# A transformer block on one core: six gates' combined weights kept in DRAM between two token blocks, and the side work of the last gates taken two steps at a time from an earlier product on

## The chip, the cores and the metric

The kernel runs on one core of one Trainium2 chip. The metric is the device time of one execution in microseconds (us). Before the change it is 3030.67 us, the median of three runs (3028.79 to 3031.12).

Engines are called as in the profile: PE (TensorE matmuls; PEld its weight loads), DVE (VectorE), ACT (ScalarE), POOL (GpSimd), SP (SyncE, which here only issues DMAs; ACT issues a few).

## The reference, cut to what matters

```python
h_x = modulate(x, norm1_g[l], sh1, sc1)                 # x: 2048 tokens x 1024
p_x = h_x @ w_in[l]                                     # w_in: 1024 x 3840, all f32
q_x, u_x, vg_x, ga_x, gb_x = jnp.split(p_x[..., KV_COLS:], REST_SPLITS, axis=-1)
...
gm_x = gmlp_spatial(jax.nn.gelu(u_x), jax.nn.gelu(vg_x), ...)
y = jax.nn.sigmoid(ga_logit) * (attn_o @ w_br_attn) + jax.nn.sigmoid(gb_logit) * (gm_o @ w_br_gm)
x = x + g1 * (y @ w_out[l])
```

The change lies in the projection `h_x @ w_in`, in its last 2048 columns, which give the two gates `ga` and `gb` (1024 columns each). Attention, the output projection and the squared-ReLU MLP come after it and are not touched.

## The kernel before, in words

**The projection.** The 2048 tokens are worked through in two token blocks of 1024 (`blk` 0 and 1, loop in `project`). Every block goes through two column pairs (`Pair`: keys, values and queries; then the gMLP's u and v) and then through eight gates (`Gate`, g = 0 to 7), each of 256 columns. Both are done by a Strassen-like scheme with seven half-size products in the order `SUMS = (0, 1, 5, 6, 4, 2, 3)`. The operands of a product are sums and differences of quarters of the block and of the weights. Every f32 operand is split in a high part `h` (rounded to fp32r) and a low part `l`, and a product is three matmuls for each 128 rows: h by h, h by l, l by h. A gate's product is 12 matmuls of 128x512 (`product`, L1609 to L1611).

**The weights of a gate.** `gate_weights(g, w)` is a generator that makes one gate's operands in steps. It loads the two 128-column halves r0 and r1 of `w_in` (L945, 512 KB each); splits r0 (ACT L954, DVE L955), which serves products 0 and 1; forms four differences (DVE L960 to L963); and splits these as two 128x1024 tiles (ACT L967, DVE L968), the first for products 5 and 3, the second for 4 and 6. Product 2's weights are loaded and split by `last_weights` (L2007, L2013, L2014) when products 5 and 6 run. The same weights serve both token blocks and are made anew in each.

**The order of the gates.** `gates` lays out the products of all gates of a run as one list: the first four products of a gate are interleaved with the last three of the gate before it. In block 1 all eight gates form one run; the list has 53 products, the first six gates in the way just told, the last two (g = 6 and 7) product by product in turn. With every product one step of the next gate's weight generator is taken, then the product is written out (`step`), then `tick` is called, once for each of the products 0 to 12 of the list and twice for each later one when `both` is true, which is in block 1 only. A gate's own evacuations are ACT copies and tanh and DVE additions on its PSUM bank (L2027, L2031, L2036, L2038, L2041, L2046, L2047); the results go to DRAM over SP (L2000). Gates 6 and 7 of block 1 keep their working tiles in the four slots named "m", all others in the eight slots named "t4".

**The side work.** `tick` takes one step of the first generator in `self.work`. These are `keys_work` (6 steps), `queries_work` (7 steps) and `mixing` (12 steps): normalization, rotary tables, gelu, the gMLP's spatial matmul (L182 to L184) and transposes, mostly on DVE and ACT. A mixing loads two tiles from DRAM (L791) into "m" slots, works on them (L802 to L833), splits (L149, L153), loads the spatial weights into an "m" slot (L839) and runs the matmuls. The "m" slots are four and one mixing fills them. In block 1 the list holds, behind what block 0 left, keys and queries of both halves and four mixings. After product 6 of gate 5 (`(g, p) == (KC - 3, 6)` in `ahead`) whatever is left of the list is written out at once. `tail` then brings in the first steps of attention (row maxima, L2100, L2106, L2111).

**Order on the engines.** The program is written with the Tile framework, whose scheduler orders each engine's instructions and hands out the slots of a tag; each engine and each DMA-issuing queue then works its instructions strictly in that order. So an instruction that waits holds up all that stand behind it on the same engine or queue.

Of the kernel before, what the change touches and what calls it, by code (L numbers as in the profile page):

```python
# [9 lines left out]
F32 = mybir.dt.float32  # L10
F32R = mybir.dt.float32r
I32 = mybir.dt.int32
AF = mybir.ActivationFunctionType
ALU = mybir.AluOpType
# [4 lines left out]
P = 128  # L19
D = 1024  # L20
KC = D // P
# [16 lines left out]
COL_GA = 1792  # L38
# [6 lines left out]
HK = KC // 2  # L45
# [5 lines left out]
def f32(ap):  # L51
    return ap.bitcast(F32)
# [10 lines left out]
}  # L63
SLOTS = {tag: n for tags in POOLS.values() for tag, n in tags.items()}
GROUP = 6
ON_VECTOR = (2, 4, 8, 14)
LAST_ON_VECTOR = (2, 4, 7, 8, 9, 12, 13, 14, 15)


class Kern:  # L70
# [119 lines left out]
    def constants(self):  # L190
        nc, I = self.nc, self.I
        ec = self.ctx.enter_context
        cp = ec(self.tc.tile_pool(name="const", bufs=1))
        dp = ec(self.tc.tile_pool(name="spill", bufs=1, space=DRAM))
        self.psum({"a": 4, "b": 4})
        self.ident = cp.tile([P, P], F32, name="ident")
        make_identity(nc, self.ident)
        self.ones = cp.tile([P, P], F32, name="ones")
        nc.vector.memset(self.ones, 1.0)
        self.lead = cp.tile([P, 1], F32, name="lead")  # L200
        nc.vector.memset(self.lead, 0.0)
        nc.vector.memset(self.lead[0:1], -1.0)
        self.G1 = cp.tile([P, KC, 2], F32, name="G1")
        self.S1 = cp.tile([P, KC, 2], F32, name="S1")
        self.G2 = cp.tile([P, KC], F32, name="G2")
        self.S2 = cp.tile([P, KC], F32, name="S2")
        self.silu = cp.tile([P, KC, 2], F32, name="silu")
        self.ss2 = cp.tile([P, SEQ // P], F32, name="ss2")
        self.gbs = cp.tile([P, GROUPS], F32, name="gbs")
        self.rg = {}  # L210
        for w in ("q", "k"):
            self.rg[w] = cp.tile([P, HD], F32, name=f"rg_{w}")

        def spill(n, shape):
            return [dp.tile(shape, F32, tag=f"{n}{b}", name=f"{n}_d{b}") for b in range(NB)]

        self.q_d = [
            [dp.tile([P, TB], F32, tag=f"q{b}_{p}", name=f"q_d{b}_{p}") for p in range(NH // 2)]
            for b in range(NB)
        ]  # L220
        self.gm_d = spill("gm", [512, TB])
        self.at_d = spill("at", [512, TB])
        self.ta_d = spill("ta", [D, TB])
        self.tb_d = spill("tb", [D, TB])
        self.x1_d = spill("x1", [TB, D])
        self.k_d = [
            [dp.tile([P, TB], F32, tag=f"k{c}_{v}", name=f"k_d{c}_{v}") for v in range(NKV)]
            for c in range(NB + 1)
        ]
        self.vc_d = dp.tile([P, TT, P], F32, tag="vc", name="vc_d")  # L230
        self.pr_d = [
            [
                [dp.tile([TB, n], F32, tag=f"p{n}_{b}_{j}", name=f"p{n}_d{b}_{j}") for j in range(2)]
                for b in range(NB)
            ]
            for n in (KVQ, TB)
        ]
        self.h_d = [
            [dp.tile([P, 2, TB], F32, tag=f"h{i}_{k}", name=f"h_d{i}_{k}") for k in range(HK)]
            for i in range(2)  # L240
        ]
        self.ws_d = [
            dp.tile([P, 2, TB], F32, tag=f"ws{c}", name=f"ws_d{c}") for c in range(2)
        ]
        self.t_d = [
            [
                [dp.tile([2, P, n], F32, tag=f"t{n}_{p}_{c}", name=f"t_d{n}_{p}_{c}") for c in range(2)]
                for p in range(7)
            ]
            for n in (KVQ, TB)  # L250
        ]

        def operands(n):
            return [
                [
                    dp.tile([2, P, TB], F32, tag=f"{n}{p}_{c}", name=f"{n}_d{p}_{c}")
                    for c in range(NCH)
                ]
                for p in range(7)
            ]  # L260

        self.ao_d = [operands(f"ao{blk}") for blk in range(2)]
        self.wo_d = operands("w2o")
        self.sm_d = spill("sm", [NH, TB])
        self.rs_d = spill("rs", [NH, TB])
        self.open("base")
        self.open("front")
# [615 lines left out]
    def context_keys(self):  # L883
# [52 lines left out]
        self.work += [self.keys_work(nt, None, kraw), self.gm_consts()]  # L936
        yield

    def gate_weights(self, g, w):
        nc = self.nc  # L940
        tt, sub = nc.vector.tensor_tensor, ALU.subtract
        lo = COL_GA + 2 * P * g
        r0, r1 = self.f4([KC, P]), self.f4([KC, P])
        for j, r in enumerate((r0, r1)):
            nc.sync.dma_start(  # L945
                r,
                self.I["w_in"][0][:, lo + j * P : lo + (j + 1) * P].rearrange(
                    "(k p) c -> p k c", p=P
                ),
            )  # L950
        b22 = r1[:, HK:]
        yield
        hr, lr = self.f4([KC, P], F32R), self.f4([KC, P], F32R)
        nc.scalar.copy(hr, r0)  # L954
        tt(out=lr, in0=r0, in1=f32(hr), op=sub)  # L955
        w[0] = [(hr[:, k], lr[:, k]) for k in range(HK)]
        w[1] = [(hr[:, HK + k], lr[:, HK + k]) for k in range(HK)]
        yield
        t13, t24 = self.f4([2, HK, P]), self.f4([2, HK, P])
        tt(out=t13[:, 0], in0=r1[:, :HK], in1=r0[:, :HK], op=sub)  # L960
        tt(out=t24[:, 0], in0=b22, in1=t13[:, 0], op=sub)
        tt(out=t13[:, 1], in0=b22, in1=r1[:, :HK], op=sub)
        tt(out=t24[:, 1], in0=r0[:, HK:], in1=t24[:, 0], op=sub)  # L963
        yield
        for alloc, t, ps in ((self.t4, t24, (5, 3)), (self.f4, t13, (4, 6))):
            h, l = alloc([2, HK, P], F32R), alloc([2, HK, P], F32R)
            nc.scalar.copy(h, t)  # L967
            tt(out=l, in0=t, in1=f32(h), op=sub)  # L968
            for i, p in enumerate(ps):
                w[p] = [(h[:, i, k], l[:, i, k]) for k in range(HK)]  # L970
            yield
    def x_block(self, b):
        return self.I["x"][0, b * TB : (b + 1) * TB]

    def gates(self, groups, begun, left, both, hook):
        n = len(groups)
        seq = []
        whole = n - 2 if both else n
        for g in range(whole):
            own = [(g, p) for p in SUMS[:4]]  # L980
            old = [(g - 1, p) for p in SUMS[4:]] if g else []
            for i in range(4):
                seq += own[i : i + 1] + old[i : i + 1]
        old = [(whole - 1, p) for p in SUMS[4:]]
        if both:
            two = [(g, p) for p in SUMS for g in (n - 2, n - 1)]
            while two:
                seq += two[:1] + old[:1]
                two, old = two[1:], old[1:]
        seq = [s for s in seq if s not in begun]  # L990
        upto = 1
        for at, (g, p) in enumerate(seq):
            if p == 0:
                for _ in groups[g].prep:
                    pass
                upto = g + 1
            elif upto < n:
                next(groups[upto].prep, None)
            groups[g].step(p)
            self.tick(1 + (both and at > 12))  # L1000
            hook(groups[g].g, p)
        left += [(groups[g], p) for g, p in old]

# [115 lines left out]
    def attend(self, units, late, mod):  # L1119
# [17 lines left out]
        for i, u in enumerate(units):  # L1137
            at = lambda n: units[n] if 0 <= n < len(units) else None
            nxt, far, old, older = at(i + 1), at(i + 2), at(i - 1), at(i - 2)
            for gi, g in enumerate(range(0, NKT, GROUP)):  # L1140
                group = range(g, g + GROUP)
                step = nxt if gi < 2 else far
                for j in group:
                    u.first(j)
                    u.second(j)
                    if j % GROUP == 2 and far and gi == 0:
                        far.load()
                    if j % GROUP == 4 and nxt and gi == 2:
                        ordered(nxt.leading)
# [11 lines left out]
                if step:  # L1161
                    step.maxima(3)
                run(4, GROUP)
                if gi == 0:
# [821 lines left out]
class Gate:  # L1986
    def __init__(self, kern, g, blk, h):
        self.k, self.nc, self.g, self.blk, self.h = kern, kern.nc, g, blk, h
        self.w = {}
        self.tag = "a"  # L1990
        ends = blk and g >= KC - 2
        self.alloc = kern.m4 if ends else kern.t4
        self.small = kern.t2 if ends and g == KC - 1 else lambda *a: kern.sb("e2", *a)
        self.prep = kern.gate_weights(g, self.w)

    def store(self, i, j, src):
        k = self.k
# [58 lines left out]
class Unit:  # L2056
# [93 lines left out]
    def second(self, j):  # L2150
        k = self.k
        c, _, ks = self.keys(j)
        if j % GROUP < GROUP - 2:
            whole = k.sb("p2", [2, TB])
# [134 lines left out]
```

## Time and profile before

| | |
|---|---|
| median of three runs | 3030.67 us |
| the profiled execution's own time | 3034.03 us |
| its span, first to last instruction | 3032.2 us |
| TensorE clock granted, mean | 0.987 |
| bytes moved by DMA | 538.59 MB |

The projection fills the first 750 us of the span, about a quarter of it; attention, the merge and the MLP follow. Block 0's gates 2 to 7 lie between 262 and 400 us, block 1's pairs between 400 and 547 us, and block 1's gates between 547 and 750 us.

In the rows of the views, "x" counts instructions, a mean is in ns, and "<-" names what an engine waited for. A row of the timeline gives start and duration in us, and in brackets the idle time before it.

### The profile page before, as it was taken

The page shows a single profiled execution, that of the slowest core. Times are in us where ns is not written, and L with a number is a line of the kernel's source. Part 1 is how long each engine was busy: PE and PEld are TensorE (multiplying, and loading weights), DVE is VectorE, ACT ScalarE, POOL GpSimd, SP SyncE. Part 2 cuts the span into 40 slices and gives each one's busy share as a digit, 9 for nine tenths or more (in the row PEclk, how much of TensorE's full clock was granted, in tenths as well). Part 3 has the DMA queues.
Part 4 walks back from the last instruction along what each step waited for, and adds up shares of the span by engine and source line. Part 5 has one row for each costly group of instructions (what it writes and reads, how often), then busy time and mean ns, then how long its engine had stood idle before and what let it go on. Part 6 is the DMA issues. An engine that isn't in the chain of part 4 may idle for free.

```text
span 3032.2 us, 37907 instructions
## 1 busy us (share of the span) xinstructions
PE 2951.8 (97%) x13325; PEld 2221.2 (73%) x13325; DVE 2088.1 (69%) x3007; ACT 1434.0 (47%) x2334; POOL 650.6 (21%) x470
## 2 busy tenths in 40 slices
PE   7989999998999999999999989999999999999999
PEld 4868788875555555555888878888887888888887
DVE  4757477876788888777655587776676766654555
ACT  5645765663554554545222255444454344444442
POOL 0000000000899899885212200000000000000000
PEclk9999999999999999999999999999999999999999
DMA  8676657654110010005767658888776544447554
GB/s 298 203 254 200 207 194 225 204 181 134 37 36 29 29 32 22 22 19 177 243 204 212 181 170 313 306 302 297 262 237 222 194 153 153 151 147 286 208 204 157
DMA packets 385440, 538.59 MB, mean 178 GB/s; under 512 B 37905, under 2 KB 196801, under 8 KB 385249
## 3 DMA queue, kind: packets, MB, share of 16 engines
q1 hardware_dynamic: 372880, 515.44, 51.6%
q10 hardware_dynamic: 12368, 20.73, 1.8%
q8 instruction: 105, 1.72, 0.2%
q14 instruction: 87, 0.70, 0.1%
HBM read 371.89 MB, written 164.10 MB: 177 GB/s over the span
## 4 chain that ended last, share of the span: by engine, by line
PE 85%; DVE 5%; DMA 5%; ACT 3%; issue 2%; SPq 0%; POOL 0%; ACTq 0%; DVEq 0%; POOLq 0%
PE b L1609 14%; PE b L1611 14%; PE b L1610 14%; PE b L2176 8%; PE b L2145 4%; PE b L2164 4%; PE b L182 4%; PE b L183 4%; PE b L184 4%; PE a L1609 3%; PE a L1610 3%; PE a L1611 3%; PE b L2100 3%; PE b L188 1%; DMA m<-in_w_in 1%
## 5 line engine op out<-in xcount | busy, mean ns | idle before, releaser
L2111 DVE TENSOR_REDUCE ts<-b 128x1 f32<-128x512 f32 x512 | 313.1, 681 | 75.4 <-PE b L2100 75.3
L2196 POOL TENSOR_TENSOR ac<-ac,p 128x512 f32<-128x512 f32 x214 | 306.4, 1465 | 55.8 <-ACT p L2168 55.8
L1725 DVE TENSOR_TENSOR b<-b,b 128x1024 fp32r<-128x1024 f32 x170 | 200.7, 1220 | 134.6 <-ACT b L1724 134.3
L1724 ACT CAST b<-b 128x1024 fp32r<-128x1024 f32 x170 | 170.7, 1051 | 222.6 <-PE b L1611 100.0
L2168 ACT ACTIVATE p<-b 128x512 f32<-128x512 f32 x384 | 194.0, 624 | 171.1 <-PE b L2164 167.9
L1610 PE MATMUL b<-b,b 128*128 128x512 f32 x680 | 265.2, 390 | 2.9 <-DVE b L1725 2.9
L1609 PE MATMUL b<-b,b 128*128 128x512 f32 x680 | 266.0, 391 | 1.6 <-DVE f L1746 1.4
L1611 PE MATMUL b<-b,b 128*128 128x512 f32 x680 | 264.7, 389 | 0.0
L2196 POOL TENSOR_TENSOR ac<-p,p 128x512 f32<-128x512 f32 x32 | 51.3, 1626 | 764.9 <-ACT p L2168 764.9
L2196 POOL TENSOR_TENSOR ac<-ac,t 128x512 f32<-128x512 f32 x152 | 204.1, 1375 | 0.0
L2145 PE MATMUL b<-h,h 128*128 128x512 f32 x576 | 188.1, 406 | 3.3 <-ACT p L2168 2.6
L2176 PE MATMUL b<-p,h 128*64 128x512 f32 x768 | 188.1, 613 | 0.0
L2164 PE MATMUL b<-h,h 128*128 128x512 f32 x576 | 179.1, 392 | 0.0
L1610 PE MATMUL b<-hb,b 128*128 128x512 f32 x446 | 173.8, 390 | 0.0
L1619 DVE TENSOR_TENSOR f<-f,b 128x512 f32<-128x512 f32 x160 | 109.1, 682 | 78.5 <-issue 45.6
L1609 PE MATMUL b<-hb,b 128*128 128x512 f32 x415 | 161.9, 390 | 0.0
L1611 PE MATMUL b<-hb,b 128*128 128x512 f32 x415 | 161.3, 389 | 0.0
L2145 PEld LDWEIGHTS b<-h,h 128*128 128x128 f32 x576 | 104.2, 189 | 64.5 <-DVE ts L2111 25.4
L1610 PEld LDWEIGHTS b<-b,b 128*128 128x128 f32 x680 | 127.7, 188 | 31.5 <-DVE b L1725 4.8
L1609 PEld LDWEIGHTS b<-b,b 128*128 128x128 f32 x680 | 127.7, 188 | 29.5 <-ACT b L1724 2.3
L1611 PEld LDWEIGHTS b<-b,b 128*128 128x128 f32 x680 | 127.6, 188 | 26.3
L1609 PE MATMUL a<-f,h 128*128 128x384 f32 (+1 forms) x320 | 119.5, 377 | 12.2 <-ACT f L634 4.8
(434 smaller groups left out, 7245.6 us busy)
## 6 DMA issues: line engine op xcount, KB each, us to landing
ao_d<-f SPq DMA_DIRECT2D x224, 256.0 KB
f<-in_w_ff SPq DMA_DIRECT2D x48, 1024.0 KB
b<-ao_d SPq DMA_DIRECT2D x85, 512.0 KB
b<-w2o_d SPq DMA_DIRECT2D x85, 512.0 KB
w2o_d<-f SPq DMA_DIRECT2D x112, 256.0 KB
f<-in_w_in SPq DMA_DIRECT2D x44, 512.0 KB
f<-x_d SPq DMA_DIRECT2D x64, 256.0 KB
hb<-ao_d SPq DMA_DIRECT2D x54, 256.0 KB
```

Of the source, the lines that this page charges most:

```text
L182: mm(ps, sh, mh, start=start, stop=False)
L1609: mm(ps, wh, hh, start=start and k == 0, stop=False, skip_group_check=True)
L1610: mm(ps, wh, hl, start=False, stop=False, skip_group_check=True)
L1611: mm(ps, wl, hh, start=False, stop=k == len(w) - 1, skip_group_check=True)
L1724: nc.scalar.copy(h, f32(l))
L1725: nc.vector.tensor_tensor(out=l, in0=f32(l), in1=f32(h), op=ALU.subtract)
L2111: nc.vector.tensor_reduce(out=self.mx[:, t, h, c : c + 1], in_=ps[h], axis=AX.X, op=ALU.max)
L2145: self.nc.tensor.matmul(self.pts[j][h], k.KA[c][self.kv][:, ks], self.qa[h], start=True, stop=False, skip_group_check=True,)
L2164: self.nc.tensor.matmul(s, k.KB[c][self.kv][:, ks], self.qb[h], start=False, stop=True, skip_group_check=True,)
L2168: self.nc.scalar.activation(pt[h], s, AF.Exp)
L2176: nc.tensor.matmul(self.o[h * HD : (h + 1) * HD, :], k.V[c][:, i, self.kv * HD : (self.kv + 1) * HD], pt[h], start=j == 0, stop=j == NKT - 1,)
L2196: nc.gpsimd.tensor_tensor(out=self.acc[e][:, h], in0=old[:, h], in1=pt[h], op=ALU.add)
```

## The change

```diff
+KEPT = 2
...
+        self.g_d = [
+            [
+                [dp.tile([P, 2, HK, P], F32, tag=f"g{g}_{n}_{i}", name=f"g{g}_d{n}_{i}") for i in range(2)]
+                for n in range(2)
+            ]
+            for g in range(KEPT, KC)
+        ]
...
+    def gate_kept(self, g, w):
+        nc = self.nc
+        lo = COL_GA + 2 * P * g
+        r0 = self.f4([KC, P])
+        nc.sync.dma_start(
+            r0, self.I["w_in"][0][:, lo : lo + P].rearrange("(k p) c -> p k c", p=P)
+        )
+        yield
+        hr, lr = self.f4([KC, P], F32R), self.f4([KC, P], F32R)
+        nc.scalar.copy(hr, r0)
+        nc.vector.tensor_tensor(out=lr, in0=r0, in1=f32(hr), op=ALU.subtract)
+        w[0] = [(hr[:, k], lr[:, k]) for k in range(HK)]
+        w[1] = [(hr[:, HK + k], lr[:, HK + k]) for k in range(HK)]
+        yield
+        for n, (alloc, ps) in enumerate(((self.t4, (5, 3)), (self.f4, (4, 6)))):
+            h, l = alloc([2, HK, P], F32R), alloc([2, HK, P], F32R)
+            for x, d in zip((h, l), self.g_d[g - KEPT][n]):
+                nc.sync.dma_start(f32(x), d)
+            for i, p in enumerate(ps):
+                w[p] = [(h[:, i, k], l[:, i, k]) for k in range(HK)]
+            yield
...
     def gate_weights(self, g, w):
...
+            if g >= KEPT:
+                keep += zip((h, l), self.g_d[g - KEPT][n])
+            for x, d in keep if n else ():
+                nc.sync.dma_start(d, f32(x))
+            yield
...
-            self.tick(1 + (both and at > 12))
+            self.tick(1 + (both and at > 4))
...
-        self.prep = kern.gate_weights(g, self.w)
+        self.prep = (kern.gate_kept if blk and g >= KEPT else kern.gate_weights)(g, self.w)
```

In block 0, gates 2 to 7 store the four split tiles of their combinations (two times h and l, 512 KB each) to DRAM, all four after the last of them is made. In block 1 these gates load the four tiles in place of r1, the four differences and the two splits; r0 is loaded and split as before, and product 2's weights are made as before. Gates 0 and 1 make their weights anew in both blocks. Apart from that, the two ticks for each product of block 1's gates begin with product 5 of the list in place of product 13.

More of the change, by code (lines that the diff above doesn't have):

```diff
@@ L964, in gate_weights @@
         yield
-        for alloc, t, ps in ((self.t4, t24, (5, 3)), (self.f4, t13, (4, 6))):
+        keep = []
+        for n, (alloc, t, ps) in enumerate(((self.t4, t24, (5, 3)), (self.f4, t13, (4, 6)))):
             h, l = alloc([2, HK, P], F32R), alloc([2, HK, P], F32R)
```

## The prediction, made before the change was run

> **What bounds the kernel now.** I read the page first, then the table of windows over the projection, then who made PE wait there, then the lines of DVE and ACT that the change takes out, and last the DMA queue.
>
> ```profile
> PE 2951.8 (97%) x13325; PEld 2221.2 (73%) x13325; DVE 2088.1 (69%) x3007; ACT 1434.0 (47%) x2334; POOL 650.6 (21%) x470
> ```
>
> Over the whole span PE is the bound. So a change that takes work from DVE and ACT can earn only what PE loses to them, and the windows say how much that is (columns: window; length; busy us of PE, PEld, DVE, ACT, POOL; granted clock; DMA share; GB/s).
>
> ```profile
> 260.00:400.00 140.00, 134.55 (x638) 109.67 (x637) 80.57 (x146) 96.37 (x147) 0.00 (x0) 1.00 0.66 215
> 400.00:547.00 147.00, 143.55 (x731) 128.28 (x730) 115.45 (x212) 87.67 (x146) 0.00 (x0) 0.99 0.63 200
> 547.00:640.00 93.00, 91.98 (x432) 75.72 (x431) 79.45 (x137) 58.26 (x90) 0.00 (x0) 1.00 0.63 195
> 640.00:700.00 60.00, 48.13 (x211) 37.98 (x210) 44.27 (x79) 31.95 (x52) 0.00 (x0) 0.94 0.52 156
> 700.00:757.00 57.00, 56.00 (x218) 35.55 (x216) 34.33 (x57) 19.25 (x36) 0.00 (x0) 0.97 0.46 150
> ```
>
> Block 1's gates are the last three rows. From 547 to 640 PE is idle 1.0 us in 93, though DVE is busy 85%; from 700 on, 1.0 us in 57. Only the 60 us from 640 to 700 are loose: 11.9 us idle, at a clock of 0.94. What ended those waits, between 560 and 700 us (total, times, longest):
>
> ```profile
> PE a L1609 <- ACT a L2047: 7.1, 2, 5.1
> PE a L1609 <- ACT t L2038: 2.7, 1, 2.7
> PE b L182 <- DMA m<-ws_d: 1.8, 3, 0.8
> PE a L1609 <- DVE t L2041: 1.2, 1, 1.2
> ```
>
> The first, second and fourth are a gate's own evacuations, late behind other work on ACT and DVE: 11.0 us. The third is a mixing's load.
>
> Why there? Four mixings run in this stretch; each ends with its spatial matmuls, whose starts are (the first row is the first load of the first mixing)
>
> ```profile
> 576.42 0.37 SPq L791 DMA_DIRECT2D m<-p_d  x1
> 608.59 0.36 PE L182 MATMUL b<-m,m 128*128 128x256 f32 x1 [0.35 <-DMA m<-ws_d]
> 636.66 0.39 PE L182 MATMUL b<-m,m 128*128 128x256 f32 x1 [0.68 <-DMA m<-ws_d]
> 665.01 0.39 PE L182 MATMUL b<-m,m 128*128 128x256 f32 x1
> 697.29 0.39 PE L182 MATMUL b<-m,m 128*128 128x256 f32 x1 [0.82 <-DMA m<-ws_d]
> 698.90 0.59 ACT L2031 COPY m<-a 128x512 f32<-128x512 f32 x1 [5.74 <-PE b L183]
> ```
>
> They come 28.1, 28.4 and 32.3 us apart, one after another, since one mixing fills the four "m" slots. The last row is gate 6's first evacuation: it needs an "m" slot and waits for the last mixing's matmuls. So the last mixing ends too late for gates 6 and 7, and what the change is worth is how much earlier it ends.
>
> **The change, part by part.** (1) Work taken out of block 1, by lines (both blocks; mean in ns):
>
> ```profile
> L960 DVE TENSOR_TENSOR f<-f,f 128x512 f32<-128x512 f32 x16 | 11.0, 689 | 14.5 <-PE a L1610 14.4
> L963 DVE TENSOR_TENSOR f<-f,f 128x512 f32<-128x512 f32 x16 | 11.0, 685 | 0.1
> L968 DVE TENSOR_TENSOR t<-f,t 128x1024 fp32r<-128x1024 f32 x16 | 19.5, 1221 | 18.3 <-PE a L1610 15.5 <-PE b L1610 1.6 <-ACT t L967 1.1
> L967 ACT CAST f<-f 128x1024 fp32r<-128x1024 f32 x16 | 16.8, 1053 | 6.8 <-DVE f L962 4.3 <-DVE f L961 1.1 <-DVE ts L172 0.8
> ```
>
> L960 to L963 are four alike, L967 and L968 two each. For one gate that is 4 x 0.687 + 2 x 1.221 = 5.19 us of DVE and 2 x 1.053 = 2.1 us of ACT; for six gates 31 us and 12.6 us. From 547 to 700 DVE was busy 79.45 + 44.27 = 123.7 of 153 us (81%) and would be at 61%. Gone as well are DVE's waits for a slot that PE holds (the idle columns of L960 and L968, 32.8 us in both blocks): DVE no longer writes those slots, SP's loads do. None of this is PE time; it pays only through the mixings and the evacuations.
>
> (2) The ticks. By product 35, where the list is emptied, before has made 13 + 2 x 23 = 59 ticks in the gates, after 5 + 2 x 31 = 67: eight steps of a mixing's twelve. The pairs give 2 ticks in each of 22 steps, 44; the list needs 98 (two mixings left over, 24; keys 12; queries 14; four mixings 48). So before is through at 44 + 13 + 2 x 20.5, product 33; after at 44 + 5 + 2 x 24.5, product 29. A gate's product is 12 matmuls, 2.72 us from the first of one to the first of the next:
>
> ```profile
> 593.57 0.39 PE L1609 MATMUL a<-hx,e 128*128 128x512 f32 x1
> 596.29 0.39 PE L1609 MATMUL a<-h,t 128*128 128x512 f32 x1
> ```
>
> Four products are 11 us earlier as written. But execution was behind the writing already (the last mixing's matmuls ran within product 41 of the list, gate 5's product 3), held by the slots, so I count on this only for the first mixing: it was written mostly one step a product and took 32 us from its first load, 576.4, to its matmuls, 608.6, against 28 for the next. Worth up to 5 us.
>
> Together: first mixing 5 us shorter; each of the next three loses most of one gate's 5.19 us from its DVE chain, I take 3. The last ends 5 + 3 x 3 = 14 us earlier, 683 in place of 697, when PE is about at gate 6's second product. Then the 11.0 us go, and the clock loss with them: 48.13 us busy at 0.94 is 2.9 us. Ceiling 13.9 us, floor 0 (what is new is priced below). I take four fifths, 11, since an in-order ACT will still be caught somewhere; what is late next is the mixings' loads, L182 behind ws_d.
>
> On the clock the trace shows
>
> ```profile
> 678.72 0.75 PE L1609 MATMUL a<-h,f 128*128 128x512 f32 x1 [2.68 <-ACT t L2038]
> 692.65 0.79 PE L1609 MATMUL a<-hx,t 128*128 128x512 f32 x1 [5.07 <-ACT a L2047]
> ```
>
> matmuls of twice the usual 0.39 us behind gaps of 2.68 and 5.07 us. [...]
>
> (3) DMA. A kept tile is 128 x 4096 B, 512 KB; block 0 stores 24 of them, 12.6 MB, block 1 loads 24 and drops six loads of r1 (3.1 MB), all on SP's queue. In 260:400 the traffic goes from 215 to 215 + 12.6 MB / 140 us = 305 GB/s; in 547:700 from (195 x 93 + 156 x 60) / 153 = 180 by 9.4 MB to about 240. What 512 KB cost the load behind it (chain: start, us, what; queue: start, issue time):
>
> ```profile
> 633.00 3.62 DMA m<-ws_d
> 387.84 4.93 DMA m<-ws_d
> 638.73 6.60 DMA m<-p_d
> 296.50 1.31 SPq L492 DMA_DIRECT2D m<-in_x  x3
> 300.50 7.25 DMA m<-in_x
> 140.00:160.00 20.00, 19.95 (x95) 16.26 (x94) 10.89 (x18) 8.89 (x16) 0.00 (x0) 1.00 0.97 312
> 160.00:180.00 20.00, 16.60 (x72) 12.92 (x71) 9.69 (x14) 5.76 (x9) 0.00 (x0) 1.00 0.85 301
> ```
>
> 512 KB alone take 3.62 us; the last of four in a row took 7.25. So each one ahead costs 1.2 us: a pair of kept loads 2.4, a burst of four stores up to 4.8. At 305 GB/s the queues are about as full as from 140 to 180 us, at 312 and 301 GB/s (share 0.97 and 0.85), where PE lost 3.45 us in 40, against 5.45 in 140 in block 0's gates. If block 0's stores brought that loss to all 140 us, they would cost 12.1 - 5.5 = 6.6 us; if no load that PE or ACT waits for stands behind a burst, nothing. I take 2: the next gate's loads follow a burst by some three products (8 us), longer than it lasts. No gain is possible, for block 0 loses no work. In block 1, four ws_d loads stand on PE's order. Were each behind a pair, 4 x 2.4 = 9.6 us; were none, nothing, or 1.8 less than now. A pair passes in 2.4 of each gate's 19 us, two pairs a gate, so about one load in four is hit, 0.6 us each, 2.4 in all, less a little for the r1 that no longer stand there; I take 2. A kept load that waits for a "t4" slot stops SP, and behind it gate results (L2000), which nobody on PE waits for, and the mixings' loads, which the 2 us hold.
>
> (4) Nothing else: the pairs, attention and the MLP keep their instructions; from 700 to 757 PE is full, and starts earlier by what was saved.
>
> **The sum.** -11 + 2 + 2 = -7.0 us: 3034.03 becomes 3027.0 for an execution like the profiled one. That one lies 3.4 us above the median; put on the median, 3023.7 us.
>
> **The rivals.** *Eaten up (about the same).* The mixings are held by their loads and the "m" slots, not by DVE: three of four cycles stay at 28 us, the last mixing ends 5 us earlier, some 4 us come back and 4 are paid. About 3030. For it: PE lost 1 us from 547 to 640 with DVE at 85%; DVE's load alone stops nothing. Against it: the last cycle, 32.3 us, holds DVE work of gate 7 (L960 to L963, L968), which is gone.
>
> *The queue (slower).* Kept tiles stand in SP's ring before loads that fixed orders wait for: r0 of six gates in each block (ACT L954), eight p_d and ws_d loads of the mixings, some twenty in all. If each comes 2.4 us later that is 48 us. A p_d load that took 6.60 us held ACT and ended in the first wait below; ACT's waits on loads in 560:700 stand under it:
>
> ```profile
> 648.59 0.50 PE L1609 MATMUL a<-hx,t 128*128 128x512 f32 x1 [2.06 <-ACT a L2047]
> ACT t L802 <- DMA m<-p_d: 4.7, 5, 2.1
> ACT f L954 <- DMA f<-in_w_in: 4.4, 3, 2.2
> ```
>
> With a third reaching PE, 16 us are paid, and the late loads halve what comes back: -5.5 + 16 = +10.5, 3041. It is slower by over 6 us from the point at which a quarter reaches PE. [...] Against it: DMA is at 0.52 from 640 to 700.
>
> *Not what it says.* The scheduler could place the kept loads so late that a product waits for its weights. A gate's weights are begun in the gate before, so a load has most of a gate's 19 us, and I give this no time of its own; its chance is in the slower case.
>
> **Chances.** 0.2%, 6 us, is what a measurement of this kernel can tell from no change. Forecast (3016 to 3028): 0.58, most of it beyond 6 us, a seventh short of it. Eaten up: 0.20. Queue: 0.22. So faster 0.50, same 0.28, slower 0.22. The range reaches from the whole ceiling with nothing paid, 3030.7 - 13.9 = 3016.8, rounded to 3016, to the slower case, 3041; the likeliest case's own is 3016 to 3028.
>
> **What would show it.** Right: L182's four starts some 25 us apart, the last near 683; no wait on L2047 or L2038 above 1 us from 640 on; DVE near 61% in block 1's gates; DMA near 305 GB/s from 260 to 400 with PE's idle there up by some 2 us. Wrong: L182 still 28 us apart (eaten up), or PE and ACT waiting longer on ws_d, p_d and in_w_in (queue), or new waits of PE on weights from the kept tiles.

## The result, and the profile after

The changed kernel takes 3018.88 us (median of six runs, 3017.04 to 3020.82), the kernel before 3030.36 us beside it (six runs, 3025.34 to 3033.76). The ratio is 0.9962, 95% interval 0.995 to 0.9975: 11.5 us faster, where 7.0 were forecast. The two profiled executions are 3034.03 us (span 3032.2) and 3019.05 us (span 3017.3). The lines named here move by 1, 9 or 37, the later in the file the more: L182 is L183, L791 is L800, L802 is L811, and L1609, L2036, L2038, L2041, L2047 are L1646, L2073, L2075, L2078, L2084.

By the page of the kernel after, 27 us of DVE and 11 us of ACT are gone:

```profile
PE 2941.9 (98%) x13325; PEld 2215.7 (73%) x13325; DVE 2061.6 (68%) x2971; ACT 1422.7 (47%) x2322; POOL 652.4 (22%) x470
```

The table of windows after (columns as in the prediction):

```profile
260.00:400.00 140.00, 134.59 (x631) 109.51 (x630) 77.19 (x140) 95.36 (x146) 0.00 (x0) 1.00 0.88 300
400.00:547.00 147.00, 142.93 (x740) 127.46 (x739) 119.99 (x219) 88.28 (x147) 0.00 (x0) 1.00 0.64 205
547.00:640.00 93.00, 90.84 (x430) 74.90 (x429) 64.84 (x118) 54.40 (x88) 0.00 (x0) 1.00 0.80 266
640.00:700.00 60.00, 53.82 (x251) 42.96 (x250) 31.88 (x62) 31.36 (x53) 0.00 (x0) 1.00 0.74 245
700.00:757.00 57.00, 56.12 (x207) 34.36 (x205) 35.86 (x59) 19.48 (x38) 5.63 (x5) 0.94 0.43 131
```

In the loose 60 us (fourth row) PE is busy 53.82 us in place of 48.13, at a clock of 1.00 in place of 0.94. The last row has POOL at work, which in the kernel before had nothing to do ahead of 757 us and all its work behind: attention has begun sooner. The first row answers the price of the stores: 300 GB/s in place of 215, and PE idle 5.41 us where it was 5.45.

What ended PE's waits from 560 to 700 us after (total, times, longest):

```profile
PE a L1646 <- ACT a L2073: 3.2, 1, 3.2
PE b L183 <- DMA m<-ws_d: 2.6, 3, 1.5
PE a L1646 <- ACT t L2075: 1.6, 1, 1.6
PE a L1646 <- DVE t L2078: 0.8, 1, 0.8
```

The evacuations cost 5.6 us in place of 11.0, the mixings' loads 2.6 in place of 1.8. The timeline shows the four mixings after (first load, then the first spatial matmul of each) and gate 6's first evacuation:

```profile
574.51 0.92 SPq L800 DMA_DIRECT2D m<-p_d  x2
602.21 0.36 PE L183 MATMUL b<-m,m 128*128 128x256 f32 x1 [0.70 <-DMA m<-ws_d]
629.84 0.38 PE L183 MATMUL b<-m,m 128*128 128x256 f32 x1 [1.46 <-DMA m<-ws_d]
655.01 0.38 PE L183 MATMUL b<-m,m 128*128 128x256 f32 x1
684.12 0.39 PE L183 MATMUL b<-m,m 128*128 128x256 f32 x1 [0.43 <-DMA m<-ws_d]
685.73 0.59 ACT L2068 COPY m<-a 128x512 f32<-128x512 f32 x1 [3.10 <-PE b L184]
```

The last mixing is 13.2 us earlier. To split that by stages I took three marks from both timelines: the first matmul of block 0's gates 2 to 7 (262.3 before, 260.9 after), the first product of block 1's gates (544.5, 542.6) and the first matmul of attention (757.0, 746.7).

| stage | before | after | difference |
|---|---|---|---|
| up to block 0's gate 2 | 262.3 | 260.9 | -1.4 |
| block 0's gates 2 to 7 and block 1's pairs | 282.2 | 281.7 | -0.5 |
| block 1's gates | 212.5 | 204.1 | -8.4 |
| the rest, where nothing was changed | 2275.2 | 2270.6 | -4.6 |

The last row is not the change's: the profiled execution before lay 3.4 us above its median. 3.9 of its 4.6 us lie in one place of attention, where six matmuls of L2100 and twelve of L2176 take 7.5 us before (from 1204.53) and 3.6 after (from 1195.88). What the change does to block 1's gates is 8.4 us, and the first three rows make 10.3 us. Each mark is of one execution, and the changed kernel profiled a second time (below) began block 1's gates 1.6 us earlier, so small differences in the first two rows say little.

### The profile page after: what moved, and what is told of

It reads as the page before. It is cut to its first block, busy times and chain, and to the rows that moved or that the text cites. A ratio compares the mean times of both kernels' runs of the same rounds, so it can differ in the third digit from the quotient of the medians.

```text
span 3017.3 us, 37910 instructions
## 1 busy us (share of the span) xinstructions
PE 2941.9 (98%) x13325; PEld 2215.7 (73%) x13325; DVE 2061.6 (68%) x2971; ACT 1422.7 (47%) x2322; POOL 652.4 (22%) x470
## 4 chain that ended last, share of the span: by engine, by line
PE 85%; DMA 5%; DVE 5%; ACT 3%; issue 2%; SPq 0%; POOL 0%; ACTq 0%; DVEq 0%; POOLq 0%
PE b L1646 14%; PE b L1647 14%; PE b L1648 14%; PE b L2213 9%; PE b L2182 5%; PE b L2201 4%; PE b L183 4%; PE b L184 4%; PE b L185 4%; PE b L2137 3%; PE a L1646 3%; PE a L1647 3%; PE a L1648 3%; PE b L189 1%; DMA m<-ws_d 1%
## 5 line engine op out<-in xcount | busy, mean ns | idle before, releaser
L1762 DVE TENSOR_TENSOR b<-b,b 128x1024 fp32r<-128x1024 f32 x170 | 200.8, 1221 | 135.9 <-ACT b L1761 135.6
L1646 PE MATMUL b<-b,b 128*128 128x512 f32 x680 | 266.2, 391 | 1.7 <-DVE f L1783 1.4
L1646 PE MATMUL b<-hb,b 128*128 128x512 f32 x415 | 161.8, 390 | 0.0
L1646 PEld LDWEIGHTS b<-b,b 128*128 128x128 f32 x680 | 127.6, 188 | 29.8 <-ACT b L1761 2.6
L1646 PE MATMUL a<-f,h 128*128 128x384 f32 (+1 forms) x320 | 119.5, 377 | 12.1 <-ACT f L643 4.9
```

The lines of the kernel that those rows point to most:

```text
L1646: mm(ps, wh, hh, start=start and k == 0, stop=False, skip_group_check=True)
L1762: nc.vector.tensor_tensor(out=l, in0=f32(l), in1=f32(h), op=ALU.subtract)
```

## The experiments

The theory is the prediction's: the last mixing ends earlier because DVE and ACT have less to do in every gate, and that lets gates 6 and 7 through. The rival "gate 7" says that only the DVE work of gate 7 matters, which lies in the last mixing's cycle. The rival "queue" says that kept tiles in SP's DMA queue (its ring, as the prediction has it) eat up part of the gain. Every ratio is to the kernel before on the same chip, with its 95% interval. The marks are the same in all kernels: start of block 1's gates, the four mixings, attention.

| kernel | median us | ratio | block 1's gates | mixings | attention |
|---|---|---|---|---|---|
| before (profile) | 3030.67 | | 544.5 | 608.6 636.7 665.0 697.3 | 757.0 |
| the change, again | 3019.96 | 0.9962 [0.9949, 0.9974] | 541.0 | 600.4 627.9 654.0 682.1 | 744.7 |
| ticks only | 3041.13 | 1.0032 [1.002, 1.0045] | 547.3 | 614.4 641.4 675.4 709.4 | 770.0 |
| kept only | 3027.34 | 0.999 [0.9981, 0.9998] | 545.7 | 608.6 636.4 661.2 688.7 | 754.2 |
| gate 7 only | 3021.79 | 0.9968 [0.9955, 0.998] | 543.5 | 607.6 636.1 664.0 689.5 | 749.1 |
| gate 7 and ticks | 3026.59 | 0.9978 [0.997, 0.9987] | 541.2 | 608.1 635.2 668.9 694.8 | 754.4 |
| stores, both blocks | 3039.78 | 1.0032 [1.0019, 1.0044] | 543.0 | 614.1 643.2 672.5 704.5 | 765.0 |
| stores, block 0 | 3026.46 | 0.9981 [0.9972, 0.9989] | 542.5 | 606.6 634.6 664.1 694.4 | 754.1 |
| POOL makes the weights | 3052.54 | 1.0067 [1.0055, 1.0079] | 545.7 | 619.5 653.3 683.2 718.7 | 780.6 |
| POOL's queue | 3028.78 | 0.9984 [0.9974, 0.9994] | 544.5 | 610.2 641.1 669.3 696.5 | 759.9 |
| own slots | 3031.09 | 0.9996 [0.9984, 1.0008] | 543.8 | 610.3 636.2 662.0 689.4 | 749.8 |
| all eight kept | 3036.48 | 1.0018 [1.0009, 1.0026] | 552.6 | 616.8 644.2 671.4 697.0 | 762.2 |
| three mixings | 3014.93 | 0.9948 [0.9936, 0.9961] | 544.8 | 609.0 637.5 666.5 | 741.5 |

The time from the start of block 1's gates to attention is the stage that the edits aim at, and the rest of the kernel varies too: the ticks alone, which touch nothing ahead of these gates, began them 2.8 us later than the kernel before. So both are read below, the median and this stage, which takes 212.5 us before and 204.1 in the change (203.7 the second time).

**The change again.** 

> The changed kernel itself, on the same chip as the next three. Both theories: 9 to 14 us faster than before, attention's first score matmul near 747 us.

Measured: -11.3 us on another chip, the mixings within 2 us of the first profile. The gain is the kernel's, not an execution's.

**The ticks alone**, in the kernel before:

```diff
-            self.tick(1 + (both and at > 12))
+            self.tick(1 + (both and at > 4))
```

> The kernel before with the ticks alone changed (two a product from product 5 of the list on); all weights are made anew in both blocks. Mixings theory (what counts is when block 1's last mixing ends, and both parts of the change bring that forward): the first mixing takes 4 to 5 us less, the others stay near 28 us, so the last mixing's spatial matmuls start near 692 in place of 697 and the time falls by 2 to 4 us. Rival, gate 7 (only the DVE work of the last gates' weights, which lay between the last mixing's steps, counts): within 1 us of before. Rival, ticks (the whole gain comes from the earlier side work): 9 to 12 us faster.

Measured: 10.7 us slower, so the expectation missed with its sign. The timeline of the ticks alone, first spatial matmul of the mixings and the two longest waits on an evacuation:

```profile
614.35 0.35 PE L182 MATMUL b<-m,m 128*128 128x256 f32 x1 [0.54 <-DMA m<-ws_d]
641.35 0.38 PE L182 MATMUL b<-m,m 128*128 128x256 f32 x1
655.88 0.80 PE L1609 MATMUL a<-hx,t 128*128 128x512 f32 x1 [3.98 <-ACT a L2047]
699.40 0.79 PE L1609 MATMUL a<-hx,t 128*128 128x512 f32 x1 [3.28 <-ACT a L2047]
709.42 0.55 PE L182 MATMUL b<-m,m 128*128 128x256 f32 x1 [5.44 <-DMA m<-ws_d]
```

Written earlier, the first mixing runs 67.1 us behind the start of the gates (64.1 before), and the third and fourth cycles take 34 us (28.4 and 32.3 before). Block 1's gates take 222.7 us, 10.2 more. So with the weights still made on DVE, an earlier place in the written order brings a mixing's steps no earlier end. My reading is that they then stand ahead of other work in the engines' order; which step holds up which was not followed. PE's own order holds the spatial matmuls ahead of a load that is not there, 5.44 us in the last row.

**The kept tiles alone**, the change without its ticks:

```diff
-            self.tick(1 + (both and at > 4))
+            self.tick(1 + (both and at > 12))
```

> The changed kernel with the ticks of before (two a product from product 13 on); gates 2 to 7 are kept in DRAM. Mixings theory: the three later mixings take 2 to 3 us less each, the first stays at 32 us, the last one's spatial matmuls start near 688 and the time falls by 5 to 8 us. Gate 7 rival: 9 to 12 us faster, as much as the whole change. Ticks rival: within 2 us of before, or slower by the DMA traffic.

Measured: 3.0 us faster, less than expected; block 1's gates take 208.5 us, 4.0 less than before. The last mixing is 8.6 us earlier than before, yet attention starts 65.5 us after it and not 59.7 as before: here PE itself is behind. One row of its timeline:

```profile
674.79 0.80 PE L1646 MATMUL a<-h,t 128*128 128x512 f32 x1 [6.14 <-ACT a L2073]
```

So the end of the last mixing is one of two bounds; the other is what PE has lost on evacuations until then.

**Gate 7 alone kept**, ticks as before:

```diff
-KEPT = 2
+KEPT = 7
```

> Gate 7's weights alone are kept in DRAM (four stores, four loads), gates 2 to 6 are made anew as before, ticks as before. Mixings theory: only the last mixing is freed of DVE work, its cycle goes from 32 to some 28 us, PE's waits on L2047 and L2038's like shrink by half, 3 to 5 us faster. Gate 7 rival: 8 to 12 us faster. Queue rival (kept tiles delay the loads that fixed orders wait for): at most 1 us is lost with so few tiles, so it says the same as the first.

Measured: 8.6 us faster, the rival's size and not mine; block 1's gates take 205.6 us, 6.9 less. The third and fourth mixing in its timeline:

```profile
663.99 0.39 PE L183 MATMUL b<-m,m 128*128 128x256 f32 x1
689.54 0.28 PE L183 MATMUL b<-m,m 128*128 128x256 f32 x1
```

The first three cycles stay as they were and the last goes from 32.3 to 25.5 us: one gate's weights, in the right place, bring three quarters of the whole change's gain with a sixth of the traffic and without the ticks. My "5.19 us of DVE in every gate, so 3 us in every cycle" is wrong as an account of where the work counts.

**Gate 7 kept, and the ticks** (the change with `KEPT = 7`).

> Gate 7's weights alone kept in DRAM, and the ticks of the change (two a product from product 5 on). The runs so far: early ticks alone made block 1's last mixing end 12 us later, gate 7 alone kept made it end 8 us earlier. If early ticks hurt as long as DVE still makes the weights of gates 2 to 6 (the mixings are then written earlier than DVE and the slots can serve them, and PE waits in order), this is 0 to 8 us slower than gate 7 alone, between -9 and 0 against before. If the early ticks help as soon as the last gates are relieved, 11 to 14 us faster than before, as the whole change or better.

Measured: 6.4 us faster, 2.2 us less than gate 7 without the ticks. The third cycle is 33.8 us again. Put together (from two chips, each against the kernel before on the same one), the earlier ticks are worth +10.7 us with no gate kept, +2.2 with gate 7 and -8.5 with gates 2 to 7 (-11.5 against -3.0). By block 1's gates alone the figures are +10.2, +7.6 (213.2 us against 205.6) and -4.4 (204.1 against 208.5): other sizes, the same order. By this stage gate 7 with the ticks gains nothing on before (213.2 against 212.5), and its 6.4 us lie outside it. The two edits of the change are not terms of a sum: among these kernels the ticks pay only where the weights of gates 2 to 7 are off DVE. Why that is so was not traced step by step.

**Stores in both blocks**: tiles stored by gates 2 to 7, and weights made anew in block 1 as before; block 1 stores as well.

```diff
-        self.prep = (kern.gate_kept if blk and g >= KEPT else kern.gate_weights)(g, self.w)
+        self.prep = kern.gate_weights(g, self.w)
```

> Block 0 stores the 24 tiles, but block 1 does not load them and makes all weights anew; ticks as before. This is the price of the stores alone: DMA in 260:400 near 300 GB/s as in the changed kernel. Mixings theory as the changed kernel's trace reads it (PE idle in block 0's gates 5.4 us both times): 0 to 2 us slower. Queue rival: 4 to 7 us slower, with PE's idle time in 260:400 up by as much.

Measured: 9.4 us slower. With stores in both blocks this prices those beside the mixings, and says nothing of block 0's alone, which the next kernel does. Of its page of windows the row of the loose 60 us, and of its waits of PE the longest:

```profile
640.00:700.00 60.00, 48.73 (x210) 38.11 (x209) 45.70 (x82) 33.92 (x53) 0.00 (x0) 0.91 0.78 267
```

```profile
PE b L183 <- DMA m<-ws_d: 7.2, 1, 7.2
```

**Stores in block 0 only**, which is the term of the prediction that was in doubt (`if g >= KEPT and not blk` ahead of the stores; block 1 and ticks as before).

> Block 0 stores the 24 tiles, block 1 makes all weights anew and stores nothing; ticks as before. (The run e4 stored in both blocks.) If the stores of block 0 cost nothing, as e4's trace has it (its block 1 gates began 1.5 us earlier than before's), within 2 us of before. If e4's 9 us came from block 0, 7 to 10 us slower.

Measured: 6.5 us faster than before, outside what was expected. The row of block 0's gates in its windows:

```profile
260.00:400.00 140.00, 135.52 (x635) 109.96 (x634) 77.90 (x141) 95.69 (x146) 0.00 (x0) 1.00 0.87 301
```

12.6 MB of stores at 301 GB/s cost PE nothing: 4.48 us idle, 5.45 before. Why it is even faster is open. Its block 1 gates take 211.6 us (212.5), 2.0 us come ahead of them, and the rest is behind the projection, where no instruction was changed. Most of that rest is the place in attention named with the result: of all profiled kernels only the one before and the own slots (below) take 7.5 us there, and whether every execution of theirs does is not known. The stores may also move the order in which the scheduler places other instructions; that this is worth several us was not shown. A median alone, 3.0 or 6.4 us off that of before, is therefore weak evidence for what an edit did; the marks of the stage carry the argument.

**All eight gates kept** (`KEPT = 0`).

> The change with all eight gates kept, in place of six: 4.2 MB more stored in block 0 and loaded in block 1, 10 us of DVE less at the start of block 1's gates, where the early ticks fall. Complement theory (early ticks pay only where DVE has room): the first mixing's matmuls come 1 to 3 us earlier, and the time is 0 to 4 us under the change's. Queue rival: the loads at the end of the pairs delay theirs, 1 to 5 us over the change.

Measured: 16.5 us slower than the change (3036.48 against 3019.96 on the same chip), 5.2 slower than before. Block 1's gates take 209.6 us, so 5.5 us are lost there; 10 us are lost before them, and here the stores have a price. Waits of PE from 20 to 260 us, the longest group of all eight kept, then the same group of the kernel after:

```profile
PE a L1646 <- ACT f L643: 15.0, 4, 5.8
```

```profile
PE a L1646 <- ACT f L643: 4.9, 2, 4.7
```

L643 splits weights that the u and v pair of block 0 has just loaded; the longest of ACT's own waits there, 6.0 us, are for tiles that are made from the loads of L606, stored and loaded again. In the timeline of all eight kept, gate 1's stores stand in SP's queue ahead of that pair's loads:

```profile
146.99 0.55 SPq L1006 DMA_DIRECT2D g_d<-f  x1
147.97 1.58 SPq L1006 DMA_DIRECT2D g_d<-t  x2
149.60 1.12 SPq L1006 DMA_DIRECT2D g_d<-f  x1
150.77 2.39 SPq L606 DMA_DIRECT2D m<-in_w_in  x2
```

From 140 to 200 us PE is busy 48.97 us here and 56.53 after, though DMA moves about as much (308 and 295 GB/s). So at about the same traffic a store was dear or free, and I put it down to who stands behind it: gates 2 to 7 load their weights a gate ahead, the pair needs its loads at once. That the stores made those loads late is read from this order; no kernel with gates 0 and 1 stored later was run, and from 140 to 160 us DMA moves 362 GB/s here and 311 after, so a fuller queue may have a part in it.

**The kept loads on POOL's queue** in place of SP's:

```diff
-                nc.sync.dma_start(f32(x), d)
+                nc.gpsimd.dma_start(f32(x), d)
```

> The whole change, but the kept tiles are loaded from POOL's DMA queue in place of SP's. If what the kept loads cost is SP's ring (the mixings' loads stand behind them in one queue, and SP stops while a kept load waits for its slot), the ws_d loads go back from 4.5-5.4 to 3.6 us and this is 2 to 5 us faster than the change. If the cost is the shared bandwidth, or nothing, within 1.5 us of the change. Slower only if the POOL queue's own issue is slow.

Measured: 4.2 us faster than before, so some 7 of the change's 11.5 us are lost. The queue rival needed a gain here. The profiled execution took 3032.43 us, 3.7 above the median; block 1's gates take 215.4 us in it. Waits of PE from 547 to 700 us, and, from its timeline, the two loads that ACT waits for in the first mixing:

```profile
PE b L183 <- DMA m<-ws_d: 10.1, 4, 4.5
PE a L1646 <- ACT t L2075: 3.6, 2, 2.9
```

```profile
576.45 0.92 SPq L800 DMA_DIRECT2D m<-p_d  x2
585.01 0.63 ACT L811 ACTIVATE t<-m 128x512 f32<-128x512 f32 x1 [4.25 <-DMA m<-p_d]
589.48 0.63 ACT L811 ACTIVATE t<-m 128x512 f32<-128x512 f32 x1 [2.31 <-DMA m<-p_d]
```

With two queues at work a p_d load is used 8.6 us after its issue; in the kernel after, with one queue, it was 5.8 us (issued at 574.51, used at 580.28). The whole mixing then runs late, and its ws_d load with it. Two things differ: the queue, and what was issued just ahead. POOL issues two kept loads at 575.00 and 575.52, ahead of the p_d load at 576.45; in the kernel after SP issues one at 572.51, ahead of it, and the next at 576.67, behind it. This run does not tell the two apart, since a load was late behind others in one queue as well: the last of four in a row on SP's took 7.25 us in the kernel before (from 300.50), one alone 3.62.

**POOL in place of DVE** for the differences and low parts of gates 2 to 7 in block 1, nothing kept (`ts` is `nc.gpsimd.tensor_tensor` for these gates; one of four differences is shown):

```diff
-        tt(out=t13[:, 0], in0=r1[:, :HK], in1=r0[:, :HK], op=sub)
+        ts(out=t13[:, 0], in0=r1[:, :HK], in1=r0[:, :HK], op=sub)
...
-            tt(out=l, in0=t, in1=f32(h), op=sub)
+            ts(out=l, in0=t, in1=f32(h), op=sub)
```

> Nothing is kept and ticks as before; in block 1 the six subtractions of the weights of gates 2 to 7 (four differences, two low parts) run on POOL, which is idle there, in place of DVE. DVE is relieved as by the change, with no DMA traffic added; ACT's two casts remain. If DVE's relief is what counts, the last mixing ends near 685 to 689 and the time falls by 8 to 12 us. If the traffic of the kept tiles ate half the gain of DVE's relief in e2, this beats e2 by 5 us or more. If it is the slots and loads that hold the mixings, or if POOL (1.4 us for 128x512 by the rows of attention, twice DVE) delivers weights late, within 3 us of before or slower.

Measured: 19.6 us slower. It takes the same work from DVE with no DMA at all, but does it slowly. The groups of POOL between 547 and 760 us, one of the low parts and one of the differences:

```profile
L969 POOL TENSOR_TENSOR f<-f,f 128x1024 fp32r<-128x1024 f32 x6 | 15.7, 2608 | 5.5 <-issue 5.2
L961 POOL TENSOR_TENSOR f<-f,f 128x512 f32<-128x512 f32 x6 | 8.3, 1379 | 609.0 <-PE b L1611 569.8 <-PE a L1611 39.2
```

2608 and 1379 ns against 1221 and 689 on DVE: twice as long. And one of its windows:

```profile
547.00:640.00 93.00, 82.36 (x365) 66.51 (x364) 71.99 (x103) 51.40 (x81) 31.27 (x17) 0.96 0.52 164
```

PE is idle 10.6 us in a stretch where it had lost 1.0. DVE is freed (71.99 us busy, 79.45 before), but here a slower chain that DVE waits for (12.1 us in two waits on POOL's low parts, from 547 to 720) cost more than the busy DVE did. This run cannot speak for or against the mixings.

**Own slots for the mixings' last stores**, so that ACT would not wait on `gm_d`; paid with one of ten "f4" slots:

```diff
-    "front": {"hx": 16, "f4": 10, "m": 4, "e2": 3},
+    "front": {"hx": 16, "f4": 9, "m": 4, "e2": 3, "go": 2},
...
-            ot = self.t2([TB])
+            ot = self.sb("go", [TB])
```

> The changed kernel, with two slots of their own for the tiles that a mixing stores at its end (they shared the six t2 slots with the gelu's), paid for with one of the ten f4 slots. In the change PE still waits 3.2 us at 668 us on a gate's copy, which stands on ACT behind a gelu step that waits for a store of the mixing before it to land (chain: gm_d<-t, 8.6 us). If that wait is what is left in the last gates: it goes, 2 to 4 us faster than the change. If the gelu's input load, which lands at about the same time, holds ACT anyway: within 1.5 us. Slower if the tenth f4 slot is needed.

Measured: as before, 11 us slower than the change. Its cycles are 26.0, 25.7 and 27.4 us, together the shortest of all with the ticks, but its first mixing comes 66.5 us after the start of the gates (59.6 in the change), and attention begins 7 us earlier than before, 5 later than in the change beside it. From attention to the end its execution takes 2279 us, the changed kernel's 2271. Of these 8 us 3.9 are the place in attention where the kernel before lost them too (7.5 us from 1199.13); what brings it about, and the other 4, I have not found. Its runs also spread from 3022 to 3038 us.

**Three mixings**, which takes the suspected bound away: the last mixing of the kernel before is left out and its part of the gMLP's result is a tile loaded once and stored twice.

> The kernel before, with the last of the eight mixings left out (its part of the gMLP's output is filled with unmixed values, so a part of the computation is missing); weights made anew and ticks as before. Mixings theory: the chain that holds gates 6 and 7 ends 32 us earlier, PE's 11 us of waits on ACT and DVE between 640 and 700 and the low clock go, and attention begins 12 to 17 us earlier (2 us of it the mixing's own PE work). Gate 7 rival (gate 7's DVE work alone makes the waits, whatever the mixings do): waits of 5 us or more stay there and it begins 3 to 7 us earlier.

Measured: 16.4 us faster than before. Its row of the loose window:

```profile
640.00:700.00 60.00, 57.39 (x267) 46.49 (x266) 36.81 (x61) 35.22 (x58) 0.00 (x0) 1.00 0.64 199
```

PE is busy 57.39 us in place of 48.13, at full clock, with all weights still made on DVE. Block 1's gates take 196.7 us, 15.8 less. So the loose stretch was the last mixing's doing, as the theory has it. The change gets 8.4 of these 15.8 us; the rest holds the last mixing's own PE work and the waits that remain. Leaving the mixing out also takes its work from DVE and ACT, so this shows that the last mixing makes the stretch loose, but not which of its steps does it.

## Why the prediction was right, and where its size was off

**The bound: right.** Attention follows the last mixing by about 60 us in before, after, ticks only, POOL's weights, both kinds of stores, both with gate 7 and own slots (59.5 to 62.6), over a spread of 37 us in the mixing's end, and by 63.5 to 65.5 in the three in which PE itself was behind (kept only, POOL's queue, all eight kept); leaving the mixing out frees the stretch.

**The mixings: right in sum, only partly in detail.** Forecast: first mixing 5 us shorter, each later cycle 3, the last at 683. Measured from the start of the gates: the first 59.6 us in place of 64.1, so 4.5 shorter; the cycles 27.6, 25.2 and 29.1 in place of 28.1, 28.4 and 32.3, so 0.5, 3.2 and 3.2; the last at 684.1. Only one cycle is near the 25 us that I named, and gate 7 alone shows that the work of one gate in one cycle can do most of it. From 547 to 700 us DVE is busy 64.84 + 31.88 = 96.7 of 153 us, 63% where 61 was forecast.

**What comes back: 9 forecast for block 1 with its loads paid, 8.4 measured.** The waits on evacuations fall by 5.4 us and the clock loss of 2.9 goes. Wrong was that no such wait above 1 us would be left. The kernel after, ACT and the PE row behind it:

```profile
662.92 1.15 ACT L811 ACTIVATE t<-m 128x512 f32<-128x512 f32 x2 [2.13 <-DMA m<-p_d]
664.27 0.63 ACT L811 ACTIVATE t<-m 128x512 f32<-128x512 f32 x1 [0.19 <-DMA m<-p_d]
664.80 1.65 ACT L815 ACTIVATE t<-t 128x512 f32<-128x512 f32 x3
666.95 0.63 ACT L811 ACTIVATE t<-m 128x512 f32<-128x512 f32 x1 [0.49 <-DMA gm_d<-t]
667.49 0.58 ACT L2073 COPY a<-t 128x512 f32<-128x512 f32 x1
668.12 0.50 PE L1646 MATMUL a<-h,t 128*128 128x512 f32 x1 [3.20 <-ACT a L2073]
```

ACT stands in a mixing's work that waits for its p_d load and for a slot that a store to `gm_d` holds; the gate's evacuation comes behind it in order, and PE waits 3.20 us. That is the catch for which the prediction took four fifths of the ceiling, though its list of signs left it out.

**The loads of block 1: 2 us forecast, 0.8 seen** as waits of PE on ws_d (1.8 to 2.6 us). What the p_d load had to do with the 3.20 us above is not in that.

**The stores of block 0: the step that failed.** For them stands "if no load that PE or ACT waits for stands behind a burst, nothing. I take 2". The traffic came as forecast (300 GB/s), the loss did not: PE idle 5.41 against 5.45 us, and the stores by themselves gave 4.48. I took PE's loss from 140 to 180 us for the price of full queues. That stretch holds the u and v pair, whose loads are needed at once, as all eight kept shows; the gates' loads are not. So this term, +2, measured nothing. With it at nothing and the loads at 0.8 the prediction's own sum is -11 + 0.8 = -10.2 us. That this is near the -10.3 of the three stages is chance: block 1's gates gave 8.4, and 1.9 lie ahead of them, 1.4 even ahead of the first of these stores, where the prediction had no gain. The last 1.2 us up to the 11.5 of the medians have no stage.

**The rivals.** "Eaten up" needed three cycles at 28 us: two of three came down. "The queue" needed longer waits on loads: SP did stand with kept loads in hand (on L965 9.5 us in five waits for PE's matmuls, from 547 to 700), but ws_d cost PE only 0.8 us more, and ACT's waits from 560 to 700 us went from 4.7 to 5.2 on p_d and from 4.4 to 1.4 on w_in; another queue made it worse. What it rightly saw is that more kept tiles are not always better: gate 7 alone -8.6, gates 2 to 7 -3.0 without the ticks, all eight with them +5.2.

**Luck in it.** The forecast added up what the two edits do. They do not add: one alone loses 10.7, the other gains 3.0, together they gain 11.5. The prediction priced the ticks at up to 5 us for the first mixing; that the sum came near is in part an accident of that.

## What to carry to other kernels

Price a store by who waits for the load behind it, and not by the share of DMA in use alone. Where several in-order engines share side work, find the last piece of it that a later stage waits for, and take work out of just that piece first: here one gate's weights gave 8.6 us, six gates' with the side work moved 11.5, and six gates' alone 3.0. Edits that move the written order and edits that take work away should be run in all four combinations, since the worth of the first can change sign with the second.

## What the runs showed of the hardware that was not expected

In the two traces of before and after the length of a gap alone did not tell whether the clock dropped behind it. In the kernel before, the 2.68 us gap that ended at 678.72 left matmuls of 0.75 and 0.63 us; in the kernel after, the gap of 3.20 us that ended at 668.12, also behind a stretch of full work, left one of 0.50 and then the usual 0.39. In the records of the granted clock of these two traces the 46 changes (27 before, 19 after) lie 3.413 us or a multiple of it apart, to within 0.001 us in each trace. Two of these steps in the kernel before, then two in the kernel after (columns as in the prediction):

```profile
675.39:678.80 3.41, 0.73 (x4) 0.27 (x3) 2.78 (x4) 3.05 (x5) 0.00 (x0) 1.00 0.28 102
678.80:682.22 3.42, 3.42 (x8) 2.70 (x9) 2.17 (x9) 0.00 (x0) 0.00 (x0) 0.50 0.02 5
```

```profile
663.07:666.48 3.41, 1.85 (x9) 1.19 (x7) 2.84 (x5) 3.20 (x6) 0.00 (x0) 1.00 0.99 387
666.48:669.90 3.42, 1.78 (x8) 1.48 (x9) 3.05 (x5) 2.95 (x5) 0.00 (x0) 1.00 0.80 324
```

The shorter gap lies whole in one step, PE is idle 2.68 us of it, and the next step runs at 0.50. The longer one is cut at 666.48 into 1.56 and 1.64 us of idle time, and the clock stays at 1.00. From the first clock record on, the two traces have 22 such steps with over 2.0 us of idle PE (2.01 to 3.41), and each was followed by one at 0.50. Idle time is not the whole account: of the steps with 1.0 to 2.0 us some were followed by 0.50 (1.89 us at 119.03 before) and some by 1.00 (1.56 us at 644.68 before), and 0.50 also came behind a step with 0.18 us (1204.46 before). What decides it these traces do not show. The prediction's ceiling, which counted a loss behind the first gap, was right to do so: 0.50 did follow the 2.68 us.

Two queues did not serve an urgent load sooner than one: with the kept loads on POOL's queue the first p_d load came 8.6 us after its issue, with all on SP's 5.8 us, though less was moved from 547 to 640 us (240 GB/s against 266). That is one pair of loads in one execution of each, with two kept loads issued just ahead of the first and one ahead of the second.
